# A two-layer hybrid decoder on one core: within-chunk products of two chunks in one block, and C B^T beside the transposed B in one PSUM bank

## The chip, the cores and the metric

The kernel runs on one core of one Trainium2 chip. A core has a matrix engine (TensorE, called PE in the profile; PEld is its loading of the stationary operand), a vector engine (VectorE, DVE), a scalar engine (ScalarE, ACT), GpSimd (POOL) and SyncE (SP), which issues most of the DMA transfers. Each engine works through its own instructions in its own order and waits for others by semaphores. Matrix products are written to PSUM, which has eight banks; a bank holds 512 float32 for each of 128 partitions. ACT and DVE read PSUM, POOL does not. The metric is the device time of one execution in microseconds (us). A profile is taken of one execution.

## The reference

One decoder layer over 512 tokens of width 1024: a layer norm, a token mixer with two branches (a Mamba-2 scan and sliding-window attention), and a SwiGLU network, each with a residual and a layer norm. The change touches the scan, which works in chunks of 128 tokens (T), with four groups (g) of eight heads (e) of width 64 (p) and a state of 128 (n):

```python
X = (xh.astype(jnp.float32) * dt[..., None]).reshape(bsz, nc, T, ng, ne, hp)
Lmat = jnp.exp(segsum(dA))
CB = jnp.einsum('bclgn,bcsgn->bcgls', Cc, Bc)
y_diag = jnp.einsum('bcgels,bcsgep->bclgep', Lmat * CB[:, :, :, None], X)
decay_states = jnp.exp(a_cum[..., -1:] - a_cum)
states = jnp.einsum('bclgn,bcgel,bclgep->bcgepn', Bc, decay_states, X)
...
_, h_in = lax.scan(step, h0, (jnp.moveaxis(states, 1, 0), jnp.moveaxis(chunk_decay, 1, 0)))
y_off = jnp.einsum('bclgn,bcgepn,bcgel->bclgep', Cc, h_in, jnp.exp(a_cum))
return (y_diag + y_off).reshape(bsz, seqlen, nh, hp)
```

y_diag is the part within a chunk; states and y_off carry the state from chunk to chunk.

## The kernel before

All large products take float32 weights split into a high and a low part, and are summed from three matrix products of 512 columns (mm3, lines 149 to 151). The split of each weight tile is an ACT cast (w_hi, L135) and a DVE subtraction (w_lo, L136). On PE the order of the instructions is that of the program text (`manual_schedule` for PE, L78). The orders of the other engines are laid out by the framework's planner from the program order and from when it expects operands to be ready.

The scan runs over 16 pairs of group and chunk, i = 4 g + c, in the loop at L947. Its small products are placed by hand between steps of large products: the Filler (L153) holds a queue of generators (projections of the next group, the gate z, the output projection of the group before), and `fill(us)` issues about that many microseconds of them. For each i the loop calls:

- ssd_pre(i + 2): loads the cumulated decays into a tile L (three buffers) by a DMA issued on SP (L746), masks it on POOL (L757) and takes eight exponentials on ACT (L762), 128x128 each.
- ssd_a(i + 1): C B^T on PE (ps_cb, L777), copied to SBUF by ACT (cb, L779) and multiplied into L by DVE (L781); four transposes of x on PE (ps_x, L784), scaled by DVE into X (L787, two buffers); and, unless it is the last chunk of a group, the transposed B on PE (ps_bt, L793), copied by ACT (bt, L795), and Xd on POOL (L798).
- fill, then the first part of ssd_b(i): the chunk's state (ps_st, L812) and what the state before it adds to y (ps_yo, L828; DVE L831; POOL L832).
- fill, then the second part of ssd_b(i): eight products X L of the chunk (ps_yd, L837; each shows in the trace as two records, 16 in all) and a DVE addition to y (L839).
- fill again.

The small products are in float32, the large ones in float32r. ps_cb, ps_x, ps_bt, ps_st, ps_yo, ps_yd and a few others share five PSUM banks (psX); a tile takes one bank whatever its size, and a new tile waits for the release of the bank that it is given. The accumulators of the large products have three banks of their own.

y of a group (y_g) has one buffer. It is still used by gate_norm of the group (L849), which runs during the first three chunks of the next group; only then does ACT start the next group's y (L774), and until then the products of that group's first chunks wait in PSUM.

Of the kernel before, what the change touches and what calls it, by code (L numbers as in the profile page):

```python
# [18 lines left out]
P = 128  # L19
# [43 lines left out]
def kernel(  # L63
# [13 lines left out]
    nc = tc.nc  # L77
# [191 lines left out]
    def axt(shape, name):  # L269
        return psX.tile(shape, F32, name=name, tag="ax")  # L270

    def acc_tile(name):
        return psA.tile([P, S], F32, name=name, tag="mm")
# [79 lines left out]
    xbc_t = {}  # L353
# [187 lines left out]
    ps = [axt([P, S], "ps_dt"), axt([P, S], "ps_k"), acc_tile("ps_v"), acc_tile("ps_q")]  # L541
# [193 lines left out]
    er = e_d.rearrange("(g j c t) l -> g c j (t l)", g=NG, j=2, c=NT)  # L735
    dt5, dec5, cd5, nac5 = cols(dtv), cols(dec), cols(cdec), cols(nac)

    z_t, y_t, yn_t, L_t, E_t, a_t, h_t = {}, {}, {}, {}, {}, {}, {}

    def ssd_pre(i):  # L740

# [22 lines left out]
    def ssd_a(i):  # L764

        g, c = divmod(i, NT)
        cs = slice(c * P, (c + 1) * P)
        b_f, c_f = xbc_t[g, 0], xbc_t[g, 1]
        xs = [xbc_t[g, 2 + t] for t in range(4)]
        if c == 0:  # L770
            y = sd.tile([P, 4, S], F32, name="y_g", tag="y_g", bufs=1)
            y_t[g] = y
            for t in range(4):
                nc.scalar.mul(out=y[:, t], in_=xs[t], mul=pc[:, C_DS + 4 * g + t:C_DS + 4 * g + t + 1])  # L774
        L = L_t[i]
        ps = axt([P, P], "ps_cb")
        nc.tensor.matmul(ps, b_f[:, cs], c_f[:, cs], start=True, stop=True)  # L777
        cb = sd.tile([P, P], F32, name="cb", tag="cb", bufs=2)
        nc.scalar.copy(out=cb, in_=ps)  # L779
        Lf = L.rearrange("p j t l -> p (j t) l")  # L780
        nc.vector.tensor_tensor(out=Lf, in0=Lf, in1=cb.unsqueeze(1).broadcast_to([P, 8, P]), op=ALU.mult)  # L781
        ps = axt([P, 4, 2, 64], "ps_x")
        for t in range(4):
            nc.tensor.transpose(ps[:, t].rearrange("p j d -> p (j d)"), xs[t][:, cs], ident)  # L784
        X = sd.tile([P, 4, 2, 64], F32, name="X", tag="X", bufs=2)
        for j in range(2):
            nc.vector.tensor_tensor(  # L787
                out=X[:, :, j], in0=ps[:, :, j],
                in1=dt5[:, g, j, c].unsqueeze(2).broadcast_to([P, 4, 64]), op=ALU.mult)
        bt = Xd = None  # L790
        if c < NT - 1:
            ps = axt([P, P], "ps_bt")
            nc.tensor.transpose(ps, b_f[:, cs], ident)  # L793
            bt = sd.tile([P, P], F32, name="bt", tag="bt", bufs=2)
            nc.scalar.copy(out=bt, in_=ps)  # L795
            Xd = sd.tile([P, 4, 2, 64], F32, name="Xd", tag="Xd", bufs=2)
            for j in range(2):
                nc.gpsimd.tensor_tensor(  # L798
                    out=Xd[:, :, j], in0=X[:, :, j],
                    in1=dec5[:, g, j, c].unsqueeze(2).broadcast_to([P, 4, 64]), op=ALU.mult)  # L800
        a_t[i] = (X, bt, Xd)

    def ssd_b(i):

        g, c = divmod(i, NT)
        cs = slice(c * P, (c + 1) * P)
        y, c_f, L = y_t[g], xbc_t[g, 1], L_t.pop(i)
        X, bt, Xd = a_t.pop(i)
        h_prev = h_t.pop(g, None)
        if c < NT - 1:  # L810
            pss = axt([P, 4, 2, 64], "ps_st")
            nc.tensor.matmul(  # L812
                pss.rearrange("p t j d -> p (t j d)"), bt, Xd.rearrange("p t j d -> p (t j d)"),
                start=True, stop=True)
            h = sd.tile([P, 4, 2, 64], F32, name="h_st", tag="h_st", bufs=2)
            h_t[g] = h
            if c == 0:
                nc.scalar.copy(out=h, in_=pss)
            else:
                for j in range(2):  # L820
                    nc.gpsimd.tensor_tensor(
                        out=h[:, :, j], in0=h_prev[:, :, j],
                        in1=cd5[:, g, j, c].unsqueeze(2).broadcast_to([P, 4, 64]), op=ALU.mult)
                nc.vector.tensor_add(h, h, pss)
        if c > 0:
            pso = axt([P, 4, P], "ps_yo")
            for t in range(4):
                nc.tensor.matmul(  # L828
                    pso[:, t], h_prev[:, t].rearrange("p j d -> p (j d)"), c_f[:, cs], start=True, stop=True)
            yo = sd.tile([P, 4, P], F32, name="yo", tag="tmp", bufs=3)  # L830
            nc.vector.tensor_mul(yo, pso, E_t.pop(i))  # L831
            nc.gpsimd.tensor_add(y[:, :, cs], y[:, :, cs], yo)  # L832
        yield
        psd = axt([P, 4, P], "ps_yd")
        for t in range(4):
            for j in range(2):
                nc.tensor.matmul(  # L837
                    psd[64 * j:64 * j + 64, t], X[:, t, j], L[:, j, t], start=True, stop=True)
        nc.vector.tensor_add(y[:, :, cs], y[:, :, cs], psd)  # L839
        yield  # L840

    def g_z(g, t):
# [99 lines left out]
    ssd_pre(0)  # L942
    ssd_pre(1)
    ssd_a(0)
    fill(4.0)
    norm = iter(())
    for i in range(NG * NT):  # L947
        g, c = divmod(i, NT)
        if c == 0 and g > 0:
            norm = gate_norm(g - 1)  # L950
            next(norm)
        if c == 0:
            add_stage(g)
        f0, f1, f2 = F_SSD[g]
        if i + 2 < NG * NT:
            ssd_pre(i + 2)
        if i + 1 < NG * NT:
            if c == NT - 1:
                all_done(f"x{g + 1}")
            ssd_a(i + 1)  # L960
        fill(f0)
        b = ssd_b(i)
        next(b)

        slots = (0, 1, 1) if g == NG - 1 else (2, 3, 4)
        fill(f1)
        for _ in range(slots.count(2 * c)):
            next(norm, None)
        next(b)
        fill(f2)  # L970
        for _ in range(slots.count(2 * c + 1)):
            next(norm, None)
        if c == NT - 1:
            all_done(f"z{g}")
            if g > 0:
                all_done(f"ya{g - 1}")
# [65 lines left out]
    for half in range(2):  # L1042
# [5 lines left out]
        for step in range(KD):  # L1048
# [4 lines left out]
            k = (4, 5, 6, 7, 1, 2, 3, 0)[step] if half else step  # L1053
# [116 lines left out]
    for f in range(2, NF):  # L1170
        pss = []
        for u in (U_FG, U_FU):
            ps = psF.tile([P, S], F32, name="ps_ff", tag="mm")
# [22 lines left out]
    for cs in (slice(0, 256), slice(256, 512)):  # L1196
        ps = psD.tile([P, 256], F32, name="ps_end", tag="dn")
# [74 lines left out]
```

## Time and profile before

| | |
|---|---|
| time, median of 3 runs (lowest to highest) | 1029.2 us (1029.1 to 1029.87) |
| the profiled execution: time, span | 1029.34 us, 1027.5 us |
| mean granted clock of PE | 0.996 |
| scan, with the projections between it | about 238 to 560 us of the span |
| ps_yd matmul records (L837) | 256, 17.5 us busy |
| ps_cb, ps_bt matmul records (L777, L793) | 32 and 12 |
| ACT copies of cb (L779) and bt (L795) | 16 of 0.244 us, 12 of 0.262 us (medians) |

Times in the views are microseconds from the start of the span. A row of the timeline is: start, duration, engine, line, operation, out<-in by the program's names, the shapes, the number of records merged, and in brackets the idle time of the engine before it with what ended it. Matmuls are pipelined, so that their durations overlap: the distance between two starts is what one costs. "Granted clock" is the share of full speed that PE was given.

### The profile page before, as it was taken

What the parts mean: (1) busy time and instruction counts of PE and PEld (TensorE: products, weight loads), DVE (VectorE), ACT (ScalarE), POOL (GpSimd) and SP (SyncE); (2) the same over time, 40 slices, a digit from 0 to 9 for tenths busy, and PEclk for the clock granted to TensorE, in tenths of its full rate; (3) what the DMA queues carried; (4) which work ended last, traced back from release to release, by engine and by line L of the source; (5) the groups of instructions that cost most, each with busy time, mean ns of one, the idle gap of its engine ahead of it and who ended that gap; (6) DMA issues with size and microseconds to landing.
All of it is one profiled execution on the core that took longest, in us unless ns stands there. A gap on an engine that the chain in (4) does not pass through costs nothing.

```text
span 1027.5 us, 13200 instructions
## 1 busy us (share of the span) xinstructions
PE 1015.6 (99%) x5044; PEld 838.2 (82%) x5044; DVE 602.2 (59%) x835; ACT 506.2 (49%) x864; POOL 206.4 (20%) x195
## 2 busy tenths in 40 slices
PE   8999999999999999999999999999999999999997
PEld 7888887887887878888888888898888888888885
DVE  6789875544656764677664595646333333332765
ACT  5464556726766885783733542434332333231450
POOL 2011213733115113111223820390000000000000
PEclk9999999999999999999999999999999999999998
DMA  8211222544444333334322344216433333331571
GB/s 317 80 65 62 87 84 103 186 147 139 136 132 113 113 117 114 119 111 137 91 93 82 128 147 177 103 42 228 141 123 123 108 118 110 116 122 62 160 250 42
DMA packets 38799, 126.56 MB, mean 123 GB/s; under 512 B 4528, under 2 KB 5040, under 8 KB 38480
## 3 DMA queue, kind: packets, MB, share of 16 engines
q1 hardware_dynamic: 36080, 116.14, 35.3%
q0 software_dynamic: 2080, 7.47, 2.0%
q10 hardware_dynamic: 576, 2.10, 0.6%
q8 instruction: 40, 0.66, 0.3%
q14 instruction: 23, 0.19, 0.1%
HBM read 119.27 MB, written 6.42 MB: 122 GB/s over the span
## 4 chain that ended last, share of the span: by engine, by line
PE 90%; DVE 2%; DMA 2%; ACT 2%; POOL 1%; issue 1%; SPq 0%; ACTq 0%; POOLq 0%; DVEq 0%
PE ps_mm L149 14%; PE ps_mm L150 14%; PE ps_mm L151 14%; PE ps_ff L151 8%; PE ps_ff L149 8%; PE ps_ff L150 8%; PE ps_da L151 2%; PE ps_da L149 2%; PE ps_da L150 2%; PE ps_mix L149 1%; PE ps_db L150 1%; PE ps_mix L151 1%; PE ps_mix L150 1%; PE ps_db L151 1%; PE ps_db L149 1%; PE ps_o L493 1%
## 5 line engine op out<-in xcount | busy, mean ns | idle before, releaser
L135 ACT CAST w_hi<-w_raw 128x1024 fp32r<-128x1024 f32 x185 | 193.3, 1051 | 306.7 <-PE ps_ff L150 120.9
L136 DVE TENSOR_TENSOR w_lo<-w_raw,w_hi 128x1024 fp32r<-128x1024 f32 x185 | 241.7, 1312 | 154.3 <-ACT w_hi L135 150.4
L149 PE MATMUL ps_mm<-hT_hi,w_hi 128*128 128x512 f32 x504 | 203.3, 403 | 0.2 <-DVE cacc L371 0.2
L150 PE MATMUL ps_mm<-hT_lo,w_hi 128*128 128x512 f32 x504 | 196.8, 391 | 0.0
L151 PE MATMUL ps_mm<-hT_hi,w_lo 128*128 128x512 f32 x504 | 196.6, 390 | 0.0
L149 PE MATMUL ps_ff<-h2T_hi,w_hi 128*128 128x512 f32 (+1 forms) x384 | 143.2, 373 | 0.0
L150 PE MATMUL ps_ff<-h2T_lo,w_hi 128*128 128x512 f32 (+1 forms) x384 | 142.6, 371 | 0.0
L151 PE MATMUL ps_ff<-h2T_hi,w_lo 128*128 128x512 f32 (+1 forms) x384 | 142.6, 371 | 0.0
L149 PEld LDWEIGHTS ps_mm<-hT_hi,w_hi 128*128 128x128 f32 x504 | 94.8, 188 | 22.3 <-issue 4.7
L151 PEld LDWEIGHTS ps_mm<-hT_hi,w_lo 128*128 128x128 f32 x504 | 94.6, 188 | 20.3
L150 PEld LDWEIGHTS ps_mm<-hT_lo,w_hi 128*128 128x128 f32 x504 | 94.9, 188 | 18.3 <-issue 1.0
L150 PEld LDWEIGHTS ps_ff<-h2T_lo,w_hi 128*128 128x128 f32 x384 | 72.3, 188 | 12.6
L151 PEld LDWEIGHTS ps_ff<-h2T_hi,w_lo 128*128 128x128 f32 x384 | 72.3, 188 | 12.5
L149 PEld LDWEIGHTS ps_ff<-h2T_hi,w_hi 128*128 128x128 f32 x384 | 72.3, 188 | 12.4
L1120 DVE TENSOR_TENSOR sgf<-sgf,ps_ff 128x512 f32<-128x512 f32 x22 | 15.1, 687 | 69.0 <-PE ps_ff L151 69.0
L149 PE MATMUL ps_mm<-yh,w_hi 128*128 128x512 f32 x124 | 49.2, 397 | 0.0
L150 PE MATMUL ps_mm<-yl,w_hi 128*128 128x512 f32 x124 | 48.3, 390 | 0.0
L151 PE MATMUL ps_mm<-yh,w_lo 128*128 128x512 f32 x124 | 48.3, 389 | 0.0
L371 DVE SCALAR_TENSOR_TENSOR cacc<-ps_mm,pc,cacc 128x511 f32<-128x511 f32 (+2 forms) x54 | 39.9, 741 | 9.9 <-ACT cacc L368 9.3
L762 ACT ACTIVATE L<-L,nac 128x128 f32<-128x128 f32 x128 | 40.9, 390 | 5.2 <-POOL L L757 5.0
L781 DVE TENSOR_TENSOR L<-L,cb 128x1024 f32<-128x1024 f32 x16 | 21.2, 1327 | 37.6 <-ACT cb L779 21.3
L757 POOL TENSOR_SCALAR_AFFINE_SELECT L<-L 128x1024 f32<-128x1024 f32 x16 | 19.1, 1194 | 93.3 <-DMA L<-a_d 86.3
(269 smaller groups left out, 1726.6 us busy)
## 6 DMA issues: line engine op xcount, KB each, us to landing
w_raw<-in_wall_dram SPq DMA_DIRECT2D x187, 512.0 KB, 3.5
L<-a_d SPq DMA_DIRECT2D x16, 512.0 KB, 5.4
E<-e_d SPq DMA_DIRECT2D x24, 128.0 KB, 3.8
x_d<-x_sb POOLq DMA_DIRECT2D x4, 512.0 KB, 7.8
row<-x_d POOLq DMA_DIRECT2D x4, 512.0 KB, 5.1
h_d<-row POOLq DMA_DIRECT2D x4, 512.0 KB, 2.9
h_r<-h_d ACTq DMA_DIRECT2D x4, 512.0 KB, 5.4
out_dram<-y_o SPq DMA_DIRECT2D x7, 256.0 KB, 4.0
```

The lines of the kernel that those rows point to most:

```text
L135: (copy or nc.scalar.copy)(out=hi, in_=w)
L136: self.last = (eng or nc.vector).tensor_sub(out=lo, in0=w, in1=hi.bitcast(F32))
L149: nc.tensor.matmul(ps, lh, rh, start=start, stop=False)
L150: nc.tensor.matmul(ps, lh, rl, start=False, stop=False)
L151: nc.tensor.matmul(ps, ll, rh, start=False, stop=stop)
L371: nc.vector.scalar_tensor_tensor(out=acc[:, d:], in0=ps[:, :S - d], scalar=pc[:, cw + 3 - d:cw + 4 - d], in1=acc[:, d:], op0=ALU.mult, op1 ...
L493: nc.tensor.matmul(ps[64 * j:64 * j + 64, n * P:(n + w) * P], v_sb[:, n, kv * 64:kv * 64 + 64], pT[:, j, 2 * n:2 * n + w].rearrange("p b k ...
L757: nc.gpsimd.affine_select(out=Lf, in_=Lf, pattern=[[0, 8], [1, P]], compare_op=ALU.is_ge, fill=-BIG, base=0, channel_multiplier=-1)
L762: nc.scalar.activation(L[:, j, t], L[:, j, t], AF.Exp, bias=nac5[:, g, j, c, t:t + 1], scale=1.0)
L781: nc.vector.tensor_tensor(out=Lf, in0=Lf, in1=cb.unsqueeze(1).broadcast_to([P, 8, P]), op=ALU.mult)
L1120: nc.vector.tensor_mul(sg, sg, pu)
```

## The change

The within-chunk products of ssd_b run only at even chunks, then for this chunk and the next: 32 records in one block, in two PSUM tiles, followed by two DVE additions. At odd chunks the second part of ssd_b is empty. ssd_a keeps C B^T and the transposed B in the two halves of one PSUM tile. The amounts of fill and the order of the other small products stay.

```diff
-        ps = axt([P, P], "ps_cb")
+
+        ps_cb = axt([P, 2, P], "ps_cb")
+        ps = ps_cb[:, 0]
         nc.tensor.matmul(ps, b_f[:, cs], c_f[:, cs], start=True, stop=True)
         cb = sd.tile([P, P], F32, name="cb", tag="cb", bufs=2)
         nc.scalar.copy(out=cb, in_=ps)
...
         bt = Xd = None
         if c < NT - 1:
-            ps = axt([P, P], "ps_bt")
+            ps = ps_cb[:, 1]
             nc.tensor.transpose(ps, b_f[:, cs], ident)
             bt = sd.tile([P, P], F32, name="bt", tag="bt", bufs=2)
             nc.scalar.copy(out=bt, in_=ps)
...
-        a_t[i] = (X, bt, Xd)
+        a_t[i], s_t[i] = (X,), (bt, Xd)
...
-        y, c_f, L = y_t[g], xbc_t[g, 1], L_t.pop(i)
-        X, bt, Xd = a_t.pop(i)
+        y, c_f = y_t[g], xbc_t[g, 1]
+        bt, Xd = s_t.pop(i)
...
         yield
-        psd = axt([P, 4, P], "ps_yd")
-        for t in range(4):
-            for j in range(2):
-                nc.tensor.matmul(
-                    psd[64 * j:64 * j + 64, t], X[:, t, j], L[:, j, t], start=True, stop=True)
-        nc.vector.tensor_add(y[:, :, cs], y[:, :, cs], psd)
+
+        if c % 2 == 0:
+            psd = [axt([P, 4, P], "ps_yd") for _ in range(2)]
+            for k in range(2):
+                X, L = a_t.pop(i + k)[0], L_t.pop(i + k)
+                for t in range(4):
+                    for j in range(2):
+                        nc.tensor.matmul(
+                            psd[k][64 * j:64 * j + 64, t], X[:, t, j], L[:, j, t], start=True, stop=True)
+            for k in range(2):
+                cs = slice((c + k) * P, (c + k + 1) * P)
+                nc.vector.tensor_add(y[:, :, cs], y[:, :, cs], psd[k])
         yield
```

More of the change, by code (lines that the diff above doesn't have):

```diff
@@ L736 @@
     dt5, dec5, cd5, nac5 = cols(dtv), cols(dec), cols(cdec), cols(nac)
-    z_t, y_t, yn_t, L_t, E_t, a_t, h_t = {}, {}, {}, {}, {}, {}, {}
+    z_t, y_t, yn_t, L_t, E_t, a_t, s_t, h_t = {}, {}, {}, {}, {}, {}, {}, {}
     def ssd_pre(i):
```

## The prediction

> **What bounds it.** I read the page's busy shares and its chain first, then the waits of PE, then the timeline of PE around one block of within-chunk products, and last the timelines of ACT, DVE, POOL and SP where C B^T is evacuated. The page:
>
> ```profile
> span 1027.5 us, 13200 instructions
> PE 1015.6 (99%) x5044; PEld 838.2 (82%) x5044; DVE 602.2 (59%) x835; ACT 506.2 (49%) x864; POOL 206.4 (20%) x195
> PE 90%; DVE 2%; DMA 2%; ACT 2%; POOL 1%; issue 1%; SPq 0%; ACTq 0%; POOLq 0%; DVEq 0%
> ```
>
> PE is busy 99% of the span and 90% of the chain that ended last. So PE's issue order is the clock of this kernel: what PE issues more cheaply is gained one for one, and what PE has to wait for is lost one for one. The other engines run behind or ahead of it with slack. The work lies between 238 us and 560 us, in the scan (ssd_pre, ssd_a, ssd_b). The profiled execution took 1029.34 us, its span and 1.8 us around it; the median of the runs is 1029.2. I make the sum from 1029.3.
>
> **The blocks.** One block of within-chunk products and its neighbours, from PE's timeline:
>
> ```profile
> 253.79 0.39 PE L151 MATMUL ps_mm<-hT_hi,w_lo 128*128 128x512 f32 x1
> 254.11 1.09 PE L837 MATMUL ps_yd<-L,X 128*64 128x128 f32 x16
> 255.13 0.50 PE L149 MATMUL ps_mm<-hT_hi,w_hi 128*128 128x512 f32 x1
> 255.47 0.40 PE L150 MATMUL ps_mm<-hT_lo,w_hi 128*128 128x512 f32 x1
> ```
>
> Starts of large products lie 0.227 us apart (254.11 would have been 254.02). From 253.79 to 255.47 pass 1.68 us; two large products account for 0.45, so the block costs 1.23. Its 16 records start 0.055 us apart (1.09 less the last one's 0.27, over 15), 0.88 in all. The rest, 0.35 us, is the switch into the block and out of it: 0.09 late at the start, the rest at the first large products after it. The change runs 16 blocks as eight of 32 records and removes one switch from each pair. One of the eight blocks that go has already no large product beside it, so I count 7.4 switches: **-2.6 us**. No matmul is added or removed. On DVE the two additions of a pair come together; DVE is 59% busy and PE does not wait for them.
>
> **What the pair needs.** The second half of a block now needs L and X of the next chunk one iteration earlier. The tightest place is the first pair of group 1:
>
> ```profile
> 317.32 2.31 DVE L781 TENSOR_TENSOR L<-L,cb 128x1024 f32<-128x1024 f32 x1
> ```
>
> L of chunk 5 is ready at 319.63. Chunk 4's block starts at 321.86 on PE, and the second half 0.88 later, so 3.1 us of cover are left. I cost this at nothing; without that cover it would be a PE wait of what is missing.
>
> **The shared bank.** This is the part that decides. Before, the transpose of B (L793) wrote a bank of its own, so PE issued it without regard to ACT's copy of C B^T (L779). Now both lie in one tile and one bank, and on PE the order is C B^T, four transposes of x, transpose of B. If accesses of two engines to one bank are kept apart, the transpose of B must wait until ACT has read C B^T, and everything behind it on PE waits too: PE is in order, and the large products stand behind it. Does the kernel keep them apart? In transposed_k, ACT (L222) and DVE (L226) read the same bank and neither needs the other's result; yet DVE waits:
>
> ```profile
> 664.53 0.55 DVE L226 TENSOR_SCALAR ln_f<-ps_tr,pc 128x256 f32<-128x256 f32 x1 [1.51 <-ACT h2T_hi L222]
> ```
>
> So an access is ordered even behind a mere read of the same bank. No row shows a PE write beside a read of other columns, which is the case here; I take it to be ordered in the same way.
>
> [...]
>
> How late is ACT's copy? Each transpose of B, and each copy of C B^T of the same chunk, in order (chunks 0, 1, 2, 4, 5, 6, 8, 9, 10, 12, 13, 14; the last chunk of a group has no transpose):
>
> ```profile
> 238.83 0.27 PE L793 MATMUL ps_bt<-ident,bc_f 128*128 128x128 f32 x1
> 240.00 0.30 PE L793 MATMUL ps_bt<-ident,bc_f 128*128 128x128 f32 x1 [0.24 <-DVE X L787]
> 262.04 0.27 PE L793 MATMUL ps_bt<-ident,bc_f 128*128 128x128 f32 x1
> 304.93 0.27 PE L793 MATMUL ps_bt<-ident,bc_f 128*128 128x128 f32 x1
> 307.81 0.27 PE L793 MATMUL ps_bt<-ident,bc_f 128*128 128x128 f32 x1
> 330.29 0.27 PE L793 MATMUL ps_bt<-ident,bc_f 128*128 128x128 f32 x1
> 377.33 0.27 PE L793 MATMUL ps_bt<-ident,bc_f 128*128 128x128 f32 x1
> 399.32 0.27 PE L793 MATMUL ps_bt<-ident,bc_f 128*128 128x128 f32 x1
> 421.31 0.27 PE L793 MATMUL ps_bt<-ident,bc_f 128*128 128x128 f32 x1
> 466.76 0.27 PE L793 MATMUL ps_bt<-ident,bc_f 128*128 128x128 f32 x1
> 489.43 0.27 PE L793 MATMUL ps_bt<-ident,bc_f 128*128 128x128 f32 x1
> 508.55 0.27 PE L793 MATMUL ps_bt<-ident,bc_f 128*128 128x128 f32 x1
> ```
>
> ```profile
> 241.56 0.24 ACT L779 COPY cb<-ps_cb 128x128 f32<-128x128 f32 x1
> 241.86 0.27 ACT L779 COPY cb<-ps_cb 128x128 f32<-128x128 f32 x1
> 271.14 0.24 ACT L779 COPY cb<-ps_cb 128x128 f32<-128x128 f32 x1
> 305.69 0.26 ACT L779 COPY cb<-ps_cb 128x128 f32<-128x128 f32 x1
> 310.55 0.24 ACT L779 COPY cb<-ps_cb 128x128 f32<-128x128 f32 x1
> 341.27 0.25 ACT L779 COPY cb<-ps_cb 128x128 f32<-128x128 f32 x1
> 381.11 0.24 ACT L779 COPY cb<-ps_cb 128x128 f32<-128x128 f32 x1
> 404.81 0.24 ACT L779 COPY cb<-ps_cb 128x128 f32<-128x128 f32 x1
> 426.95 0.25 ACT L779 COPY cb<-ps_cb 128x128 f32<-128x128 f32 x1
> 469.25 0.24 ACT L779 COPY cb<-ps_cb 128x128 f32<-128x128 f32 x1
> 493.03 0.24 ACT L779 COPY cb<-ps_cb 128x128 f32<-128x128 f32 x1
> 512.74 0.24 ACT L779 COPY cb<-ps_cb 128x128 f32<-128x128 f32 x1
> ```
>
> End of the copy less start of the transpose: 2.97, 2.13, 9.34, 1.02, 2.98, 11.23, 4.02, 5.73, 5.89, 2.73, 3.84 and 4.43, together **56.3 us** for which PE would stand. Why is the copy late? It is queued on ACT behind the eight exponentials of a later chunk, which come from ssd_pre and stand earlier in the program. For chunk 12:
>
> ```profile
> 458.83 1.09 PE L837 MATMUL ps_yd<-L,X 128*64 128x128 f32 x16
> 459.96 0.38 SPq L746 DMA_DIRECT2D L<-a_d  x1
> 464.99 1.09 POOL L757 TENSOR_SCALAR_AFFINE_SELECT L<-L 128x1024 f32<-128x1024 f32 x1 [2.69 <-DMA L<-a_d]
> 466.89 2.45 ACT L762 ACTIVATE L<-L,nac 128x128 f32<-128x128 f32 x8
> ```
>
> The block of chunk 10 frees a buffer of L (there are three), the load is issued at once, lands 5 us later, then come the mask and the exponentials, and then the copy. This chain starts at the block and does not care that PE stands, so the wait stays, with two corrections. For even chunks the buffer is free after the first half of a pair, and the second half then stands between it and the transpose: 0.88 less in seven of them (2 to 14), -6.1. For odd chunks the buffer that the later exponentials need was freed a whole iteration earlier, by the pair; those exponentials should be done. The four odd rows hold 14.7; their bounds are nothing and 14.7, and I take 0.7 each, nearest to the row of chunk 4 (1.02), whose copy had no exponentials ahead: -11.9. That leaves **+38.3 us**; its ends are nothing (every copy prompt) and 56.3.
>
> **The clock.** PE stands for microseconds now. Once in this trace it does something like it, at the start:
>
> ```profile
> 12.91 0.78 PE L217 MATMUL ps_tr<-ident,x_sb 128*128 128x128 f32 x2 [1.08 <-ACT x_sb L563]
> 15.30:18.80 3.50, 3.50 (x14) 2.92 (x15) 3.47 (x6) 2.68 (x4) 0.00 (x0) 0.54 1.03 405
> ```
>
> After an idle microsecond in sparse work the granted clock (the 0.54 in the second row, a stretch of 3.5 us) is about half; that costs 1.6 us. I count it for the three longest stalls (chunks 2, 6 and 10): **+4.8 us**; ends nothing and twelve times, 19.
>
> [...]
>
> Sum: 1029.3 - 2.6 + 38.3 + 4.8 = 1069.8, so **1070 us**.
>
> **Rivals.** *Prompt copies.* The order on ACT is laid out anew; if the copy of C B^T goes ahead of the exponentials, as at chunk 4, the wait shrinks to what ACT is busy with. The balance point is 2.6 / 12 = 0.22 us for each transpose: below it the change is no loss. With half of that, 0.1 each, the time is 1029.3 - 2.6 + 1.2 = 1027.9. For it: chunk 4. Against: the seven even chunks keep their order and the time between the block and the copy. If some copies move ahead and others not, the time lies between 1030 and 1050.
>
> *No wait at all.* The two halves count as separate, or the transpose is not ordered behind the copy: 1029.3 - 2.6 = 1026.7. Against it stands DVE's idle time behind ACT's read.
>
> *Banks.* The tile of a block of group 1 is held until its y_g exists:
>
> ```profile
> 372.82 0.69 DVE L839 TENSOR_TENSOR y_g<-y_g,ps_yd 128x512 f32<-128x512 f32 x1 [1.50 <-ACT y_g L774]
> ```
>
> Chunk 4's products, done at 322.9, sit in PSUM until 372.8. With the pair two of five banks are held from there, a whole iteration earlier than now, and ps_yo may wait for a bank, as the transpose of chunk 1 does in the list above (0.24 behind DVE's X): some 0.7 us over three groups. Without stalls the time would be 1029.3 - 2.6 + 0.7 = 1027.4; beside them it is lost in their spread.
>
> **Numbers.** A measurement of this kernel can tell about 0.2% (2.1 us) from no change. Stalls in most of the twelve places, 1050 to 1096 us: 0.62. Stalls in some, 1030 to 1050: 0.20. Prompt copies or no wait: 0.13, of which 0.06 below 1027.1 and 0.07 about equal. Above 1096, where the stalls keep their full 56 us and more of them drop the clock: 0.05. The range from 1030 to 1096 holds 0.82. Faster 0.06, same 0.07, slower 0.87.
>
> **What would show it.** Right: PE waits, in the view of waits, for ACT cb L779 at ps_bt, twelve times and some 35 to 40 us in all, the longest at chunks 2 and 6; the granted clock falls below 1.0 in some stretch between 240 and 560 us; eight blocks of 32 records. The blocks' part is wrong if a block of 32 takes more than 1.8 us. The stall's part is wrong if PE shows no idle time before L793 of the old numbering, or if ACT's copies stand ahead of the exponentials. It would be wrong in size if the odd chunks wait as long as before.

## The result, and the profile after

The changed kernel takes 1077.44 us (median of 4 runs, 1075.64 to 1078.93) against 1029.5 us before (4 runs): 1.0469 times as long, 95% interval 1.0457 to 1.0481. The profiled execution took 1076.54 us, 47.2 us more than that of before. The page of the changed kernel, with PE's shares, the chain that ended last and one group of instructions:

```profile
span 1074.8 us, 13197 instructions
PE 1026.4 (95%) x5044; PEld 848.5 (79%) x5044; DVE 610.1 (57%) x835; ACT 495.0 (46%) x854; POOL 207.8 (19%) x195
PE 86%; ACT 5%; DMA 4%; DVE 2%; issue 2%; SPq 0%; POOL 0%; ACTq 0%; DVEq 0%
L795 PE MATMUL ps_cb<-ident,bc_f 128*128 128x128 f32 x12 | 4.6, 385 | 38.1 <-ACT cb L781 38.1
```

PE was busy for 99% of the span and is now for 95%. Nearly all that is missing stands in one group: before the transposed B (now L795), PE was idle for 38.1 us, all of it behind ACT's copy of C B^T (now L781). On the chain that ended last, ACT and DMA rose from 2% each to 5% and 4%: most of it is the exponentials, and the loads of L, ahead of that copy. PE's waits name the same place:

```profile
PE ps_cb L795 <- ACT cb L781: 38.1, 10, 6.3
```

(total, number, longest). One of the ten, chunk 2, on PE's timeline and on ACT's:

```profile
263.74 0.38 PE L779 MATMUL ps_cb<-bc_f 128*128 128x128 f32 x2
263.96 0.60 PE L786 MATMUL ps_x<-ident,xs_f 128*128 128x128 f32 x4
270.62 0.47 PE L795 MATMUL ps_cb<-ident,bc_f 128*128 128x128 f32 x1 [6.06 <-ACT cb L781]
...
271.32 0.63 PE L150 MATMUL ps_mm<-hT_lo,w_hi 128*128 128x512 f32 x1
271.75 0.63 PE L151 MATMUL ps_mm<-hT_hi,w_lo 128*128 128x512 f32 x1
```

```profile
263.33 1.28 ACT L762 ACT_TABLE_LOAD   x1 [0.61 <-DMA L<-a_d]
264.63 2.15 ACT L762 ACTIVATE L<-L,nac 128x128 f32<-128x128 f32 x7
266.79 1.28 ACT L375 ACT_TABLE_LOAD   x1
268.08 0.63 ACT L375 ACTIVATE xs_f<-cacc 128x512 f32<-128x512 f32 x1
268.71 1.28 ACT L762 ACT_TABLE_LOAD   x1
270.01 0.40 ACT L762 ACTIVATE L<-L,nac 128x128 f32<-128x128 f32 x1
270.32 0.25 ACT L781 COPY cb<-ps_cb 128x128 f32<-128x128 f32 x1
```

C B^T is complete at 264.1, but ACT first takes the eight exponentials of a later chunk, which waited for their load, with an activation of another kind and two table loads among them; the copy comes at 270.32. PE stands from the last transpose of x until 270.62. And when it goes on, large products start 0.43 us apart instead of 0.23. The reason is in the windows of the changed kernel (stretch, length, busy time of PE, PEld, DVE, ACT, POOL with instructions, granted clock, DMA share, GB/s); the first is an undisturbed one:

```profile
255.00:262.00 7.00, 7.00 (x55) 5.67 (x55) 5.79 (x8) 4.30 (x7) 1.45 (x2) 1.00 0.69 210
269.80:276.70 6.90, 6.08 (x15) 4.84 (x16) 1.23 (x1) 4.13 (x13) 0.00 (x0) 0.51 0.00 0
321.00:324.50 3.50, 3.50 (x17) 3.50 (x17) 2.46 (x3) 2.63 (x11) 0.78 (x1) 0.51 0.07 26
351.80:358.60 6.80, 5.01 (x13) 3.95 (x14) 1.23 (x1) 4.23 (x12) 1.20 (x3) 0.50 0.00 0
454.20:461.00 6.80, 5.71 (x14) 4.55 (x15) 1.23 (x1) 4.04 (x13) 0.00 (x0) 0.50 0.00 0
505.30:512.20 6.90, 3.44 (x9) 2.77 (x10) 2.96 (x3) 5.90 (x18) 0.00 (x0) 0.51 0.23 76
556.50:559.90 3.40, 3.40 (x10) 2.61 (x9) 2.98 (x5) 3.37 (x5) 2.12 (x2) 0.51 0.00 0
```

After six of the ten waits (chunks 2, 4, 6, 10, 12 and 14) PE was granted half its speed, for 3.4 us or twice that. Last, a block of a pair:

```profile
255.27 0.39 PE L151 MATMUL ps_mm<-hT_hi,w_lo 128*128 128x512 f32 x1
255.59 1.97 PE L843 MATMUL ps_yd<-L,X 128*64 128x128 f32 x32
257.49 0.50 PE L149 MATMUL ps_mm<-hT_hi,w_hi 128*128 128x512 f32 x1
257.82 0.40 PE L150 MATMUL ps_mm<-hT_lo,w_hi 128*128 128x512 f32 x1
```

From 255.27 to 257.82 pass 2.55 us; less two large products (0.45) the block costs 2.10, against twice 1.23 before.

Where the 47.2 us lie: from the first C B^T to the first product of the output projection PE's timeline has 373.1 us before (238.2 to 611.3) and 421.5 after (236.9 to 658.4), 48.4 more. Of these 38.1 are the waits; 11.2 are the 56 large products at half clock, 0.2 us each; the eight pairs give back 2.9; some 2.0 are left for small products at half clock and the restart after each wait. Ahead of the scan the changed kernel was 1.3 us earlier: before has a stretch of half clock at 15 us (0.54 from 15.30 to 18.80), which this execution does not have.

### The profile page after: what moved, and what is told of

It reads as the page before. It is cut to its first block, busy times and chain, and to the rows that moved or that the text cites. A ratio compares the mean times of both kernels' runs of the same rounds, so it can differ in the third digit from the quotient of the medians.

```text
span 1074.8 us, 13197 instructions
## 1 busy us (share of the span) xinstructions
PE 1026.4 (95%) x5044; PEld 848.5 (79%) x5044; DVE 610.1 (57%) x835; ACT 495.0 (46%) x854; POOL 207.8 (19%) x195
## 4 chain that ended last, share of the span: by engine, by line
PE 86%; ACT 5%; DMA 4%; DVE 2%; issue 2%; SPq 0%; POOL 0%; ACTq 0%; DVEq 0%
PE ps_mm L149 14%; PE ps_mm L150 14%; PE ps_mm L151 13%; PE ps_ff L151 7%; PE ps_ff L150 7%; PE ps_ff L149 7%; DMA L<-a_d 3%; PE ps_da L151 2%; PE ps_da L150 2%; PE ps_da L149 2%; ACT L L762 2%; PE ps_mix L149 1%; PE ps_mix L150 1%; PE ps_mix L151 1%; PE ps_o L493 1%
## 5 line engine op out<-in xcount | busy, mean ns | idle before, releaser
L136 DVE TENSOR_TENSOR w_lo<-w_raw,w_hi 128x1024 fp32r<-128x1024 f32 x185 | 245.6, 1332 | 202.0 <-ACT w_hi L135 200.0
L149 PE MATMUL ps_mm<-hT_hi,w_hi 128*128 128x512 f32 x504 | 206.9, 411 | 0.0
L150 PE MATMUL ps_mm<-hT_lo,w_hi 128*128 128x512 f32 x504 | 200.5, 398 | 0.0
L151 PE MATMUL ps_mm<-hT_hi,w_lo 128*128 128x512 f32 x504 | 199.9, 397 | 0.0
L149 PEld LDWEIGHTS ps_mm<-hT_hi,w_hi 128*128 128x128 f32 x504 | 97.7, 194 | 22.1 <-issue 3.4
L151 PEld LDWEIGHTS ps_mm<-hT_hi,w_lo 128*128 128x128 f32 x504 | 96.9, 192 | 21.1
L150 PEld LDWEIGHTS ps_mm<-hT_lo,w_hi 128*128 128x128 f32 x504 | 97.3, 193 | 19.3 <-issue 1.0
L795 PE MATMUL ps_cb<-ident,bc_f 128*128 128x128 f32 x12 | 4.6, 385 | 38.1 <-ACT cb L781 38.1
L834 POOL TENSOR_TENSOR y_g<-y_g,yo 128x512 f32<-128x512 f32 x12 | 15.5, 1292 | 119.4 <-DVE yo L833 62.7
```

Of the source, the lines that this page charges most:

```text
L136: self.last = (eng or nc.vector).tensor_sub(out=lo, in0=w, in1=hi.bitcast(F32))
L149: nc.tensor.matmul(ps, lh, rh, start=start, stop=False)
L150: nc.tensor.matmul(ps, lh, rl, start=False, stop=False)
L151: nc.tensor.matmul(ps, ll, rh, start=False, stop=stop)
```

## The experiments

The theory to be tried: PE waits because a read of the shared bank stands between its two writes, and the read is late because it is queued behind the exponentials. The rivals: that the pair itself loses the time (two PSUM banks held earlier, L and X needed earlier), that the shared bank as such costs, and that the clock has nothing to do with the waits.

**Pairs, but a bank each** (e1).

```diff
-        ps_cb = axt([P, 2, P], "ps_cb")
-        ps = ps_cb[:, 0]
+        ps = axt([P, P], "ps_cb")
...
-            ps = ps_cb[:, 1]
+            ps = axt([P, P], "ps_bt")
```

> The products run in pairs as in the changed kernel, but C B^T and the transposed B have a bank each again. Theory (the loss is the wait of the transpose for ACT's copy of C B^T): the wait is gone, eight switches of PE are saved, so 1029.5 - 2.6 = 1026.9 us, and no PE wait behind ACT cb. Rival (the loss comes from the pair: two PSUM banks held a whole iteration earlier, L and X needed earlier): about 1077 us or more, with PE waits behind DVE at ps_yo, ps_bt or ps_yd; if the pair takes part of it, something between.

1029.63 us against 1028.67: 1.0007 (0.9998 to 1.0015), the same. The 38 us are gone with the shared bank, so the pair is not what loses them. But the pair's gain isn't there either, and PE's waits say why:

```profile
PE ps_yo L829 <- ACT cb L780: 2.5, 1, 2.5
...
PE ps_bt L794 <- DVE yo L832: 1.4, 1, 1.4
```

ps_yo reads nothing of cb: it waits for a bank. This is at chunk 5, where the pair of chunks 4 and 5 holds two of the five banks; the other wait lies among the crowded small products before that pair. Together PE stands 3.9 us for banks that ACT and DVE have not yet emptied, and a stretch of half clock (0.50 from 339.56 to 342.97) follows the longer wait; the pairs save 2.9.

**The shared bank alone**, products chunk by chunk (e2; the edits of ps_cb and ps_bt from the change, nothing else of it).

> The shared bank alone; the products run chunk by chunk as before. Theory: the wait is there, and it is longer than in the changed kernel, since the odd chunks' exponentials are not ahead of time: the changed kernel's 38 us and some 11 us more for chunks 1, 5, 9 and 13, with the clock term and without the 2.6 us saved: 1077 + 2.6 + 11 = about 1090 us. Rival (the pair makes the loss): 1029.5 us.

1091.79 us: 1.0613 (1.0599 to 1.0628).

```profile
PE ps_cb L794 <- ACT cb L780: 44.3, 11, 7.9
```

The shared bank makes the whole loss, and more of it than in the changed kernel: the waits of chunks 5, 9 and 13 are 1.9, 5.3 and 4.0 us here, and 0, 0.9 and 0.4 there; at chunks 9 and 13 of the changed kernel the exponentials are done by then, since the pair frees the buffer of L an iteration earlier. Other places go the other way (chunk 4 waits 0.9 us here and 4.7 there), and nine stretches of half clock follow in place of six (mean granted clock 0.976 against 0.983).

**Both writes first** (e3): the changed kernel with one line moved.

```diff
         nc.tensor.matmul(ps, b_f[:, cs], c_f[:, cs], start=True, stop=True)
+        if c < NT - 1:
+            nc.tensor.transpose(ps_cb[:, 1], b_f[:, cs], ident)
         cb = sd.tile([P, P], F32, name="cb", tag="cb", bufs=2)
         nc.scalar.copy(out=cb, in_=ps)
...
             ps = ps_cb[:, 1]
-            nc.tensor.transpose(ps, b_f[:, cs], ident)
```

> Pairs and shared bank as in the changed kernel; only the transpose of B is issued on PE right behind C B^T, ahead of ACT's copy in the program, so that both writes of the bank come before both reads. Theory (PE waits because a read of the bank stands between its two writes): no PE wait, 1026.9 us. Rival (the shared bank itself costs, through its longer hold or through contention of PE and ACT): clearly above 1029.5 us. The copy of C B^T may start 0.06 us later; it is off the path.

1025.16 us against 1028.67: 0.9964 (0.9951 to 0.9978). This is 0.36% faster than the kernel before, and so beats both kernels. The gain is 3.5 us where 2.6 were expected: the blocks give 2.9, and 0.7 us of small waits that the kernel before has at ps_yo and ps_bt (0.5 and 0.2 behind DVE's X) are gone here. PE at chunk 2:

```profile
261.51 0.38 PE L779 MATMUL ps_cb<-bc_f 128*128 128x128 f32 x2
261.73 0.27 PE L781 MATMUL ps_cb<-ident,bc_f 128*128 128x128 f32 x1
261.84 0.60 PE L788 MATMUL ps_x<-ident,xs_f 128*128 128x128 f32 x4
262.19 0.47 PE L149 MATMUL ps_mm<-hT_hi,w_hi 128*128 128x512 f32 x1
```

No idle time at the transpose; ACT's copies are as late as ever (at chunk 2 at 269.15, 7 us after this transpose), and nobody on PE asks for them. So neither the shared bank nor the pair costs: the read between the writes does.

**The exponentials behind the copy** (e4): ssd_a(i + 1) called before ssd_pre(i + 2).

```diff
-        if i + 2 < NG * NT:
-            ssd_pre(i + 2)
         if i + 1 < NG * NT:
...
             ssd_a(i + 1)
+        if i + 2 < NG * NT:
+            ssd_pre(i + 2)
```

> The changed kernel, with ssd_pre(i + 2) called after ssd_a(i + 1) instead of before it, so that the eight exponentials stand behind the copy of C B^T in the program. Theory (the wait is long because the copy is queued behind the exponentials on ACT): each wait falls to what ACT is busy with, 0.1 to 1 us in ten places, 3 us at chunk 0 (there the y_g scalings are ahead), no half clock in the scan: 1027 + 3 + 5 = about 1035 us. Rival (the copy is late for another reason, such as ACT's casts or table loads): still over 1060 us.

1046.47 us: 1.0174 (1.0160 to 1.0188). The waits fell from 38.1 to 15.3 us. Chunk 2 on PE, and then chunk 5 on ACT:

```profile
266.56 0.33 PE L795 MATMUL ps_cb<-ident,bc_f 128*128 128x128 f32 x1 [0.34 <-ACT cb L781]
```

```profile
316.46 0.63 ACT L863 ACTIVATE sq<-y_g 128x512 f32<-128x512 f32 x1 [2.38 <-DVE y_g L861]
317.06 1.24 ACT L866 ACTIVATE s<-y_g 128x512 f32<-128x512 f32 x2
318.20 0.25 ACT L781 COPY cb<-ps_cb 128x128 f32<-128x128 f32 x1
```

At chunk 2 the wait fell from 6.06 to 0.34, and so it did, to between 0.3 and 0.9, at chunks 4, 6, 8, 10 and 14, and at chunk 12 from 5.51 to 1.82; chunks 9 and 13 stay at 0.9 and 0.4, and chunk 0 at 2.86. But chunk 5 waits 6.40 now: its copy is queued behind squares of gate_norm, which wait for DVE. The exponentials are what made the copy late at most places; what PE waits for is whatever ACT has in front of it. The expectation of 1035 missed this place and the half clock (0.50) behind it and behind chunk 0.

**More PE work inside the waits** (e5, e8). The product C B^T is issued several times over where PE would stand; the values are the same.

```diff
-        nc.tensor.matmul(ps, b_f[:, cs], c_f[:, cs], start=True, stop=True)
+        for _ in range({2: 45, 4: 34, 6: 45, 10: 45, 12: 40}.get(i, 1)):
+            nc.tensor.matmul(ps, b_f[:, cs], c_f[:, cs], start=True, stop=True)
```

> The changed kernel, with the product C B^T of chunks 2, 4, 6, 10 and 12 issued 45, 34, 45, 45 and 40 times over (the same values into the same columns), so that PE works through some 4 to 5 us of the time in which it would stand; 204 products more, at 0.11 us each some 22 us of added PE work. Theory of the clock (the stalls cost more than their idle time, because PE is granted half speed afterwards): the added work lies within the waits, the half clock after five of the six places goes, and the kernel gets faster, by about 10 us: 1077 - 10 = 1067 us, with PE's idle time behind ACT cb down by about 22 us, from 38 to 16. Rival (the half clock has nothing to do with the waits): 1077 us, with the half clock where it was. If the added work isn't covered by the waits: up to 1099 us.

1084.5 us: 1.0534 (1.0520 to 1.0548). I had taken a product for 0.11 us; it is two records of 0.11, so that 45 us were added and overfilled the waits. PE's waits at the transpose were 10.1 us, 28 fewer, so 17 us should have been added to the time; 7 were, and all but one of the stretches of half clock were gone (mean granted clock 0.997 against 0.983). The same with the counts 22, 17, 23, 22 and 20:

> The run with added products again, now sized by what one of them took there (two records of 0.11 us, 0.22 us a product): C B^T of chunks 2, 4, 6, 10 and 12 is issued 22, 17, 23, 22 and 20 times, 99 products more, 22 us of added PE work that fits inside the waits of the changed kernel at those places (6.1, 4.7, 6.3, 6.0 and 5.5 us). Theory of the clock: PE's idle time behind ACT cb falls by 22 us from 38 to 16, five of six stretches of half clock go, and with them about 11 us: 1077.4 - 11 = 1066 us, with more work than before. Rival (the half clock is no consequence of the waits, or costs nothing): 1077 us.

1070.49 us: 1.0397 (1.0382 to 1.0413), 7 us less than the changed kernel with 22 us more PE work.

```profile
PE ps_cb L796 <- ACT cb L782: 18.4, 11, 3.4
```

```profile
266.00:272.50 6.50, 5.01 (x45) 4.78 (x44) 2.02 (x4) 6.46 (x14) 2.38 (x4) 1.00 0.26 83
...
401.90:405.30 3.40, 3.40 (x10) 2.67 (x9) 0.23 (x1) 1.54 (x7) 0.00 (x0) 0.51 0.02 5
```

Work and waits together are 22 + 18.4 - 38.1 = 2.3 us more, the time is 6.9 less: 9 us are the clock's. At the five places that were filled it stays at 1.00. The sixth, chunk 14, was not filled and waits 3.44 us here, and it too stays at 1.00; and two stretches of half clock appeared after chunks 0 and 8, whose waits (2.86 and 2.40 us) are those of the changed kernel. What went with them stands in the last section. The expected 1066 was missed by these two stretches and by 2.4 us more of waits.

**Shared bank and both writes first, but no pairs** (e6; the line moved as in e3, in the kernel of e2).

> The shared bank with both PE writes ahead of the reads, as in the run that was faster, but products chunk by chunk as before. Theory (the pair's eight switches carry the gain): no PE wait at the transpose, 1028.7 us, or 0.5 to 1 us less, since one bank less in use takes away the small waits behind DVE's X (0.5 and 0.2 us). Rival (the shared bank carries the gain of 3.5 us): 1025 to 1026 us.

1028.22 us against 1029.27: 0.9993 (0.9984 to 1.0001). The shared bank alone is worth nothing that these runs can tell from noise; the gain needs the pairs.

**Pairs, both writes first, but a bank each** (e9; e3 with a tile ps_bt of its own).

> Pairs, the transpose of B right behind C B^T, but in a bank of its own. It tells apart why the pairs gained 3.5 us with a shared bank and nothing without. Bank theory (the pair holds two of five banks for long, and one tile less is what frees PE from waiting for a bank): PE waits at ps_yo, ps_x or ps_bt of 2 to 4 us in all, 1028 to 1030 us. Order rival (the earlier transpose makes the gain): 1025.2 us and no such waits.

1028.67 us against 1029.15: 0.9994 (0.9985 to 1.0003).

```profile
PE ps_x L788 <- DVE yo L833: 2.0, 1, 2.0
PE ps_yo L830 <- ACT cb L783: 1.8, 1, 1.8
...
PE ps_x L788 <- DVE X L791: 0.7, 1, 0.7
```

4.5 us of waits for banks stand where e3 has none. So the pair's gain needs the bank that sharing frees; order alone doesn't give it.

**Fewer changes between small and large products** (e7): e3, with the first part of ssd_b (the state and what it adds to y; at the last chunk of a group the latter alone) moved beside other small products in ten places.

```diff
             ssd_a(i + 1)
+        b = ssd_b(i)
+        early = c == 3 or (g == 0 and c == 1)
+        late = c == 0 or (g == 0 and c == 2)
+        if early:
+            next(b)
         fill(f0)
-        b = ssd_b(i)
-        next(b)
+        if not early and not late:
+            next(b)
...
+        if late:
+            next(b)
         next(b)
         fill(f2)
```

> The faster version (pairs, shared bank, both writes first), with the state products of ssd_b moved next to other small products in ten of the sixteen places: beside the block of the pair in chunk 0 of each group and chunk 2 of the first group, beside C B^T of the next chunk in chunk 3 of each group and chunk 1 of the first group. The fill amounts stay. If a switch between small and large products costs 0.35 us wherever it is: ten fewer, 1025.2 - 3.5 = 1021.7 us. If tiles of PSUM are then held back to back so that PE waits for a bank: above 1023.5 us, with PE waits behind DVE or ACT at ps_yo, ps_x or ps_yd.

1025.17 us: 0.9965 (0.9952 to 0.9979), the same as e3. State and block side by side at chunk 0:

```profile
251.54 0.39 PE L151 MATMUL ps_mm<-hT_hi,w_lo 128*128 128x512 f32 x1
251.76 1.02 PE L815 MATMUL ps_st<-Xd,bt 128*128 128x512 f32 x2
252.71 1.97 PE L844 MATMUL ps_yd<-L,X 128*64 128x128 f32 x32
254.61 0.50 PE L149 MATMUL ps_mm<-hT_hi,w_hi 128*128 128x512 f32 x1
254.95 0.40 PE L150 MATMUL ps_mm<-hT_lo,w_hi 128*128 128x512 f32 x1
```

From 251.54 to 254.95 pass 3.41 us; less two large products (0.45), 2.96 are left. Apart, in e3, the state costs 0.88 and the block 2.10, 2.98. Nothing is saved. The state has no such 0.35 us of its own to save: its two records start 0.43 us apart, which is 0.86 of its 0.88. So the 0.35 us are not a price of going from large to small products. They go with the block of within-chunk products itself (the one whose stationary operand is 128x64), whatever stands beside it, and joining two such blocks saves them once. Which property of the block makes them is not shown. One place of this run is worse: at chunk 4 the second half of the block, at 321.66, comes 0.87 us late, for L of chunk 5 is ready only at 321.56.

## Why the prediction was right

**The blocks.** -2.6 forecast; 16 blocks of 1.23 became eight of 2.10, which is -2.9. The size held, the reason was too wide: I called it a switch between large and small products, and e7 shows that it belongs to the block. For the same reason the block that I counted as costing less is no exception. By one sign that I had set, a block of 32 over 1.8 us, this part would be wrong, for the row reads 1.97. The sign was: with my own figures, 31 distances of 0.055 and the last record's 0.27, a block of 32 had to read 1.97.

**What the pair needs.** Right for the changed kernel: PE has no wait at ps_yd there, since PE itself runs later. Without those waits the cover of 3.1 us is used up: in e3 L of chunk 5 is ready at 321.50, the second half of chunk 4's block was due at 321.28, and that block takes 2.30 us in place of 1.97.

**The shared bank.** Right in mechanism and in sum: 38.3 forecast from twelve places, 38.1 measured in ten. e1 and e3 show that it is the read between the writes, and e2 that it does not need the pair. The sign of twelve waits named ps_bt was met as ten, under the name ps_cb. DVE waiting 1.51 us behind ACT's read of one bank, the row on which I rested it, was the right sign: in the changed kernel PE's write waits behind ACT's read of other columns of the same tile, with 6.06 us of idle time for it at chunk 2. The profile infers what ended a wait from semaphores, so this is an order that the program keeps; whether it is kept by tile or by bank no run separates, since each tile has a bank to itself. The single places were less good than their sum. Chunks 2 and 6, forecast at 8.5 and 10.4, waited 6.06 and 6.34; chunk 4, at 0.1, waited 4.68, for now exponentials stood ahead of its copy, and chunk 12, at 1.9, waited 5.51, for a cast, an activation and two table loads came in between its exponentials. The correction for odd chunks held: 1.3 us in all, 2.8 forecast. That the errors cancel to 0.2 us is luck.

**The clock.** The term that was mis-sized: 4.8 us for three stalls, where six were followed by half clock, with 34 us in all at half speed and 11.2 us lost on the large products alone. I had taken one stretch of 3.5 us for each; two of the six lasted 3.41 us and four 6.83. e5 and e8 show that the stretches go with the waits: at the five places that e8 filled with work the clock stays at 1.00, and 9 to 10 us come back. Nor did it take one of the longest stalls: half clock followed chunk 14's wait of 2.93 us here, and not chunk 0's of 2.86. With 13.2 (11.2, and the 2.0 for small products and restarts) in place of 4.8 the sum would have been 1078.2; 1077.44 was measured.

**The rivals.** Prompt copies: e4 shows that what speaks against it was right (the copies are queued), and that even with the exponentials out of the way the wait stayed above the balance of 0.22 us in eleven of twelve places. No wait at all: refuted by the ten waits. Banks: 0.7 us forecast. In the changed kernel no such wait is left, because sharing frees a bank; with a bank each it is 3.9 us (e1) and 4.5 (e9), more than the pair gains. I had not seen that the two halves of the change need each other.

## What to carry to other kernels

When two results of the matrix engine share a PSUM tile (here one bank), issue both writes before anyone reads either: with a read between them PE waited here for all that ACT had queued ahead of it, 38.1 us over ten places, and moving one line turned 1077.4 into 1025.2 us. Before a wait is added to the engine that bounds the kernel, subtract in the profile the end of the new releaser from the start of the new waiter, place by place, and allow for the clock as well: here half clock came after six of the ten waits, those of 4.68 to 6.34 us and one of 2.93, and lost another 11.2 us on the large products. A change that holds buffers longer and one that frees a buffer may each be worth nothing alone (e6, e9) and 0.36% together (e3).

## What was not expected of the hardware

Half clock did not simply follow the length of a wait. It came after 2.93 us at chunk 14 of the changed kernel and not after 2.86 at chunk 0; in e8 it came after 2.86 and 2.40 us at chunks 0 and 8, and not after 3.44 at chunk 14. In the trace of the changed kernel the six stretches start at 269.84, 321.04, 351.76, 454.16, 505.36 and 556.56; the second and the last are 3.413 us long, the others 6.827. They begin between 2.11 us (chunk 12) and 5.28 us (chunk 2) after PE began to wait, so in this run they keep no fixed distance to the waits. The distances between their starts are 51.20, 30.72, 102.40, 51.20 and 51.20 us, which is 15, 9, 30, 15 and 15 times the 3.413 us of a short one. I therefore laid windows of this length on the starts, in the changed kernel (chunk 0, then chunk 14) and in e8 (chunk 0, then chunk 14):

```profile
239.12:242.53 3.41, 1.96 (x12) 1.68 (x13) 1.65 (x3) 2.31 (x7) 1.72 (x2) 1.00 0.78 222
553.15:556.56 3.41, 1.00 (x5) 0.87 (x6) 3.11 (x5) 3.17 (x11) 0.00 (x0) 1.00 0.00 0
556.56:559.97 3.41, 3.41 (x10) 2.62 (x9) 2.92 (x5) 3.38 (x5) 2.16 (x2) 0.50 0.00 0
```

```profile
238.15:241.56 3.41, 0.72 (x7) 0.72 (x7) 2.14 (x3) 2.99 (x8) 2.16 (x2) 1.00 0.84 152
241.56:244.97 3.41, 3.41 (x11) 2.61 (x10) 0.76 (x2) 2.71 (x7) 1.67 (x2) 0.50 1.05 279
545.35:548.76 3.41, 1.79 (x11) 1.35 (x10) 2.56 (x4) 3.30 (x7) 0.98 (x1) 1.00 0.36 127
548.76:552.17 3.41, 1.60 (x8) 1.34 (x9) 3.23 (x5) 3.17 (x10) 0.00 (x0) 1.00 0.00 0
552.17:555.58 3.41, 3.41 (x17) 2.83 (x16) 2.33 (x4) 3.38 (x6) 2.17 (x2) 1.00 0.03 10
```

The 2.86 us at chunk 0 of the changed kernel fall into two windows, with 1.41 (from 235.71 to 239.12) and 1.45 us idle, and the clock stays at 1.00; at chunk 14 one window is idle for 2.41, and the next has 0.50. In e8 it is the other way round: 2.69 us in one window at chunk 0, with 0.50 in the next, and 1.62 and 1.81 in two at chunk 14, with 1.00. So in these four places half clock went with the idle time within one window, and not with the length of the wait. Over the changed kernel up to 1000 us of its span, the windows ahead of the six stretches are idle for 2.11 to 3.41 us, and of the others at full clock none for more than 1.87; yet the stretch at 15 us of the kernel before came behind a window with 1.83, so that these traces give no limit. The four long stretches of the changed kernel have 0.77 to 3.40 us idle in their first window, the two short ones none. This was read off the traces afterwards, and no run was made to try it.

And the 0.35 us around a block of products with a 128x64 stationary operand did not shrink when the block's neighbour was another small product: state and block cost 2.96 us side by side in e7, and 2.98 apart in e3.
